# Layer 0's recurrence on pairs of chunks, memory attention on two row halves, an earlier page table and a new order in a two-layer decoder step

## The chip, the cores and the metric

The kernel runs on one core of a Trainium2 chip. The metric is the time of one execution on the device in microseconds (us). Of the kernel before three runs were timed, and one further execution was recorded by the profiler. TensorE is called PE below and its weight loads PEld; VectorE is DVE, ScalarE is ACT, GpSimd is POOL, and SyncE is SP.

## The reference

One step of a decoder with two layers, for a prompt of 512 tokens and 8 samples of 4 tokens (544 columns in all). Layer 0 mixes tokens by a gated linear recurrence, layer 1 by attention over keys that an indexer selects; beside the mixer each layer attends with 4 heads to 256 memory tokens, and each layer ends with a gated MLP that has a convolution over three tokens. The recurrence, which the change rewrites, is by chunks of 32 tokens and heads of 128:

```python
HGRN_CHUNK = 32
def step(S, inp):
    qc, kc, vc, gc = inp
    b = jnp.cumsum(gc, axis=2)
    b_last = b[:, :, -1:, :]
    q_dec = qc * jnp.exp(b)
    k_dec = kc * jnp.exp(-b)
    scores = jnp.where(causal, jnp.einsum('bhtk,bhsk->bhts', q_dec, k_dec), 0.0)
    o = jnp.einsum('bhtk,bhkv->bhtv', q_dec, S) + jnp.einsum('bhts,bhsv->bhtv', scores, vc)
    S_new = (jnp.exp(b_last[:, :, 0, :])[..., None] * S
             + jnp.einsum('bhsk,bhsv->bhkv', kc * jnp.exp(b_last - b), vc))
    return S_new, o
```

Six such heads stand side by side, the prompt has 16 chunks in each, and the state after the last chunk is an output too.

## The kernel before

Activations lie feature-major in tiles of 128 rows and 544 columns (32 of the samples, then 512 of the prompt). The weights come as 199 units of 128x1024, loaded by SP's queue up to three units ahead. `Weights._cut` splits each into two parts: `whi` by ACT, and `wlo` (the rest) by DVE or by POOL, whichever a planner's clock finds free. A projection (`fm`, `proj_fm`, `mm3`) adds three products of the parts, so the groups `a<-hi,whi`, `a<-lo,whi` and `a<-hi,wlo` make up most of PE's work. Every instruction is issued by one helper, so nearly all carry the same line, L398; they are told apart by the names of the tiles that they write and read.

The order of the instructions is not written out by hand. The program is a main line of projections with Python generators beside it (`Pump`), each a piece of work that yields what it must wait for. A planner (`Model`) keeps a clock for each engine by estimated costs, and decides between two main-line products which generator goes on; priorities stand in `PRI`, thresholds in `MAIN0`, `LEAD0`, `SLACK` and `BUSY`, and the main line of layer 0 in `MIX`: a number is a head's two projections, "hi" the values of two heads, "mem" the keys and values of the memory (`mkv` on PE), "g" a gate.

The parts that the change touches:
- `hgrn_head`, one generator for each of the six heads. A block is 128 tokens, that is 4 chunks; a head has 4 blocks. `front` makes the block's scores (`sc`) and the turned keys and then, on DVE, `km`: four masked copies of those, one for each chunk. `middle` makes 4 products `u` of 128x128 with all 128 rows at work, of which the mask leaves 32, and steps the state four times on DVE (`st`). `back` makes the output `ho`: the masked scores times the values, plus for each chunk the queries times the state before it, a product on 32 columns of PE. `ot` and `ots` turn the normed output.
- `mem_prompts`: four generators, each for two heads of memory attention and two tiles of tokens. The scores `ms` use 64 rows of PE (the head's 64 features). Then come the softmax, the turn `mpt` and the product `mo` into 64 columns.
- `out_proj` and `Norm`: the output projection adds into the stream `x`; behind each of its 8 feature blocks come `hi`, `lo`, a square and the sum `sqa`. `Norm._finish` sums the squares over features on PE (`st__finish`), takes the inverse root by 13 small DVE instructions (`m__finish`, `rs`), and spreads it by 5 PE transposes (`rb__finish`); the MLP's first results can only leave PSUM after that.
- The page table of layer 1's cache: 9 small DMAs issued on ACT's queue into `ptb` and `ptv`, and DVE instructions that turn them into row numbers (`iidx`, `vidx`). They stand in the program behind `out_proj`.

In the profile each full float32 product is two passes, so `u_hgrn_head ... x8` is 4 products.

## Time and profile before

| | us |
|---|---|
| median of 3 runs | 1495.1 |
| lowest and highest run | 1492.55, 1497.12 |
| span of the profiled execution | 1500.7 |
| PE busy in it | 1434.9 (96%), 11314 passes |
| DVE, ACT, POOL busy | 803.2, 587.5, 567.3 |
| mean granted clock of PE | 0.98 |

The profiled execution has no other time than its span, which is 5.6 us over the median. Busy PE means that some matmul was under way: ends of matmuls are modelled, so a stretch with a cold clock is busy too. The granted clock is the share of full speed (1.00 is 2.4 GHz, 0.50 is 1.2 GHz). Layer 0's mixer runs from the start to about 340 us, its MLP to about 700, layer 1's mixer to about 1100, and its MLP to the end.

### The profile page before, as it was taken

The page shows a single profiled execution, that of the slowest core. Times are in us where ns is not written, and L with a number is a line of the kernel's source. Part 1 is how long each engine was busy: PE and PEld are TensorE (multiplying, and loading weights), DVE is VectorE, ACT ScalarE, POOL GpSimd, SP SyncE. Part 2 cuts the span into 40 slices and gives each one's busy share as a digit, 9 for nine tenths or more (in the row PEclk, how much of TensorE's full clock was granted, in tenths as well). Part 3 has the DMA queues.
Part 4 walks back from the last instruction along what each step waited for, and adds up shares of the span by engine and source line. Part 5 has one row for each costly group of instructions (what it writes and reads, how often), then busy time and mean ns, then how long its engine had stood idle before and what let it go on. Part 6 is the DMA issues. An engine that isn't in the chain of part 4 may idle for free.

```text
span 1500.7 us, 28191 instructions
## 1 busy us (share of the span) xinstructions
PE 1434.9 (96%) x11314; PEld 1345.6 (90%) x11314; DVE 803.2 (54%) x1762; ACT 587.5 (39%) x1064; POOL 567.3 (38%) x600
## 2 busy tenths in 40 slices
PE   8989999998999999999999797689999999999998
PEld 7978889998999999999987775456999999999998
DVE  7466886653444234444469988867444442244431
ACT  5447466332333123333335443466333331133320
POOL 4422444323444124446753444341134440144410
PEclk9999999999999999999999997989999999999999
DMA  5542132321333223224414236631222323232241
GB/s 186 177 156 64 59 117 86 101 85 62 88 95 93 92 73 94 90 85 126 135 54 131 83 115 202 199 127 57 71 76 89 96 85 99 73 95 87 85 121 57
DMA packets 60145, 152.52 MB, mean 102 GB/s; under 512 B 9040, under 2 KB 22960, under 8 KB 60016
## 3 DMA queue, kind: packets, MB, share of 16 engines
q1 hardware_dynamic: 39456, 110.11, 23.9%
q0 software_dynamic: 8208, 26.50, 5.4%
q10 hardware_dynamic: 12352, 14.13, 2.9%
q8 instruction: 89, 1.46, 0.4%
q14 instruction: 40, 0.33, 0.1%
HBM read 142.23 MB, written 8.47 MB: 100 GB/s over the span
## 4 chain that ended last, share of the span: by engine, by line
PE 84%; DVE 11%; issue 2%; ACT 1%; DMA 1%; another core or an unknown queue 0%; ACTq 0%; POOL 0%; SPq 0%; DVEq 0%; POOLq 0%
PE a L398 71%; DVE ple_choose_sample L398 2%; PE u_hgrn_head L398 1%; DVE isc_index_prompt L398 1%; PE id_index_prompt L398 1%; PE mkv L398 1%; PE ao_prompt_attn L398 1%; PE ho_hgrn_head L398 1%; PE ms_prompt L398 1%; PE hgrn_head_samples L398 1%; PE as_prompt_attn L398 1%; DVE t L398 1%; DMA ptv<-pt 1%; DVE lo L398 1%; PE mo_prompt L398 1%
## 5 line engine op out<-in xcount | busy, mean ns | idle before, releaser
L398 PE MATMUL a<-hi,whi 128*128 128x272 f32 x2640 | 556.4, 292 | 1.4 <-DVE t L398 1.0
L398 PE MATMUL a<-lo,whi 128*128 128x272 f32 x2640 | 551.0, 290 | 4.9 <-DVE lo L398 4.6
L398 POOL TENSOR_TENSOR wlo<-raw,whi 128x1024 fp32r<-128x1024 f32 x143 | 342.7, 2397 | 557.3 <-ACT whi L398 551.1
L398 PE MATMUL a<-hi,wlo 128*128 128x272 f32 x2640 | 549.1, 289 | 0.0
L398 PEld LDWEIGHTS a<-hi,whi 128*128 128x128 f32 x2640 | 417.7, 190 | 9.2 <-issue 5.4
L398 PEld LDWEIGHTS a<-lo,whi 128*128 128x128 f32 x2640 | 418.1, 190 | 6.2 <-DVE lo L398 5.6
L398 PEld LDWEIGHTS a<-hi,wlo 128*128 128x128 f32 x2640 | 418.1, 190 | 0.0
L398 ACT ACTIVATE whi<-raw 128x1024 fp32r<-128x1024 f32 (+1 forms) x202 | 209.5, 1038 | 230.9 <-PE a L398 151.3
L398 DVE TENSOR_TENSOR wlo<-raw,whi 128x1024 fp32r<-128x1024 f32 (+1 forms) x59 | 79.7, 1351 | 160.6 <-ACT whi L398 157.7
L398 DVE TENSOR_TENSOR sc<-a,rb 128x544 f32<-128x544 f32 x53 | 38.4, 724 | 116.1 <-PE a L398 114.5
L398 DVE SCALAR_TENSOR_TENSOR conv<-ext,params,conv 128x560 f32<-128x560 f32 x88 | 70.6, 802 | 45.1 <-ACT conv L398 43.6
L398 DVE TENSOR_TENSOR ext<-a,rb 128x240 f32<-128x240 f32 x132 | 37.5, 339 | 105.9 <-PE a L398 102.2
L398 ACT ACTIVATE conv<-ext,params 128x560 f32<-128x560 f32 x44 | 37.6, 855 | 136.2 <-DVE ext L398 132.6
L398 ACT ACTIVATE hi<-sc 128x544 fp32r<-128x544 f32 x44 | 29.0, 658 | 137.3 <-DVE sc L398 137.3
L398 DVE TENSOR_TENSOR x<-a,x 128x544 f32<-128x544 f32 x48 | 34.7, 723 | 80.1 <-PE a L398 72.5
L398 POOL TENSOR_TENSOR sqa<-sqa,sq 128x544 f32<-128x544 f32 x24 | 34.8, 1448 | 110.0 <-ACT sq L398 108.3
L398 DVE TENSOR_TENSOR sc<-sc,conv 128x512 f32<-128x512 f32 x88 | 62.5, 748 | 4.9 <-DVE sc L398 0.5
L398 ACT ACTIVATE conv<-conv 128x560 f32<-128x560 f32 x44 | 29.6, 672 | 73.8 <-DVE conv L398 73.8
L398 ACT ACTIVATE hi<-x,params 128x544 fp32r<-128x544 f32 x32 | 23.9, 745 | 70.4 <-DVE x L398 68.5
L398 DVE TENSOR_TENSOR lo<-sc,hi 128x544 fp32r<-128x544 f32 x44 | 31.9, 725 | 31.9 <-ACT hi L398 31.9
L398 PE MATMUL a<-whi,hi 128*128 128x256 f32 x160 | 46.8, 293 | 0.0
L398 PE MATMUL a<-whi,lo 128*128 128x256 f32 x160 | 45.1, 282 | 0.0
(406 smaller groups left out, 1931.9 us busy)
## 6 DMA issues: line engine op xcount, KB each, us to landing
raw<-w SPq DMA_DIRECT2D x177, 512.0 KB, 3.6
raw<-w POOLq DMA_DIRECT2D x21, 512.0 KB
k_sample_scores<-ckT SPq DMA_DIRECT2D x46, 128.0 KB, 3.5
ck_mem_samples<-cmkT ACTq DMA_DIRECT2D x16, 256.0 KB, 6.2
cv_mem_samples<-cmv ACTq DMA_DIRECT2D x16, 256.0 KB, 4.7
st_s<-hgrn_head_samples POOLq DMA_DIRECT2D x12, 256.0 KB
hgrn_head_samples<-hst SPq DMA_DIRECT2D x10, 256.0 KB, 3.5
ck_sample_scores<-ckT SPq DMA_DIRECT2D x18, 128.0 KB, 2.1
```

Of the source, the lines that this page charges most:

```text
L398: return f(*args, **kw)
```

## The change

**Recurrence.** `hgrn_head` keeps states for pairs of chunks (64 tokens): 8 states for a head instead of 16. The masked copies `km` are gone. `updates` makes two products per block, of rows 0 to 63 and of rows 64 to 127, which write two PSUM banks. `scores` has one more product (`k` by the second chunk's queries, 128x64) for the part inside a pair, and three more ACT copies. `outputs` works on two blocks at a time. Instructions of the six heads: `u` 96 to 48, DVE state steps 96 to 48, `km` 24 to none, ACT copies of 32x32 none to 48 and of 128x128 (`kt`) none to 24, `o` copies 24 to 12.

**Memory attention.** In layer 0 both heads of a generator make their scores in turn, on the two row halves and into two banks; in both layers `mo` takes the heads in turn.

**Page table.** The 9 DMA issues go ahead of head 3's projections, the DVE instructions ahead of `out_proj`.

**Order.** New constants for the planner in layer 0; in layer 1 and its MLP the old order is replayed from a written string (`SCRIPT`), and PE's rows there differ in `mo` alone. Who makes `wlo` changes too: DVE 59 to 33 of the units, POOL 143 to 169; the 26 that change hands are all in layer 0. In all, PE goes from 10445 to 10415 instructions, DVE from 1671 to 1593, ACT from 1003 to 1062, POOL from 605 to 629.

```diff
-KEEP, MAIN0, MAIN1 = 3, 5, 1
+KEEP, MAIN0, MAIN1 = 3, 1, 1
-LEAD0, LEAD1, POOLED = -1.0, -100.0, 0
+LEAD0, LEAD1, POOLED = -3.0, -100.0, 1
-MIX = "0 hi hi mem 1 2 3 4 hi 5 g g g g g g".split()
+MIX = "0 1 hi mem 3 4 hi 2 5 hi g g g g g g".split()
...
+            def scores(*es):
+                for e in es:
+                    sbs[e] = bank("ms")
+                for i in range(2):
+                    for e in es:
+                        T.matmul(sbs[e][:, 256 * i:256 * i + 256], tok(qs[j][0], 2 * tp + i)[prs[e], :],
+                                 kt[prs[e], 256 * j:256 * j + 256], start=True, stop=True, skip_group_check=True)
...
+            for es in [(0, 1)] if l == 0 else [(0,), (1,)]:
...
-        def front(blk):
-            cols = slice(NS + 128 * blk, NS + 128 * blk + 128)
-            sb = bank("sc")
-            T.matmul(sb[:, 0:128], kd[:, cols], q[:, cols], start=True, stop=True, skip_group_check=True)
-            T.transpose(sb[:, 128:256], k[:, cols], ident)
-            sc = scs[blk % 3]
-            V.copy_predicated(sc, cc("bcaus").bitcast(I32), sb[:, 0:128])
-            km = slot(name="km")
-            V.tensor_mul(v3(km[:, :512], 4, 128), sb[:, 128:256].unsqueeze(1).to_broadcast([128, 4, 128]),
-                         cc("cmask").unsqueeze(2).to_broadcast([128, 4, 128]))
-            st[blk] = sc, km
...
+        def scores(blk, sb):
+            cols = slice(NS + 128 * blk, NS + 128 * blk + 128)
+            T.matmul(sb[:, 0:128], kd[:, cols], q[:, cols], start=True, stop=True, skip_group_check=True)
+            T.matmul(v3(sb[:, 256:320], 2, 32), k[:, cols], v3(q[:, cols], 2, 64)[:, :, 32:64], start=True, stop=True,
+                     skip_group_check=True)
+            T.transpose(sb[:, 128:256], ku[:, 128 * blk:128 * blk + 128], ident)
+            sc = scs[blk % 3]
+            V.copy_predicated(sc, cc("bcaus").bitcast(I32), sb[:, 0:128])
+            for p in range(2):
+                S.activation(sc[64 * p:64 * p + 32, 64 * p + 32:64 * p + 64], sb[64 * p:64 * p + 32, 256 + 32 * p:288 + 32 * p], AF.Copy)
+            kt = kts[:, 128 * blk:128 * blk + 128]
+            S.activation(kt, sb[:, 128:256], AF.Copy)
+            st[blk] = sc, kt
...
+        def updates(blk, ub):
+            for p in range(2):
+                rows = slice(64 * p, 64 * p + 64)
+                T.matmul(ub[p], st[blk][1][rows], vv(blk)[rows], start=True, stop=True, skip_group_check=True)
...
+        scores(0, bank("sc"))
+        for n in range(1, 5):
+            yield [kts] if n != 3 else [kts, st[1][1]]
+            hb = bank("ho") if n == 3 else None
+            b = bank("sc" if n < 4 else "ho")
+            ub = b[:, 384:512], bank("u")[:, 0:128]
+            updates(n - 1, ub)
+            if n == 3:
+                outputs(0, hb)
+            if n < 4:
+                scores(n, b)
+            scan(n - 1, ub)
...
+        if hd == 3:
+            page_table()
...
+        pump.begin(SCRIPT)
```

VectorE at the end of layer 0's mixer, before: the last blocks of `out_proj`, the page table's row numbers, and the norm.

```order
L398 TENSOR_TENSOR x_89<-a_3986,x_89 128x544
L398 SCALAR_TENSOR_TENSOR lo_4037<-x_89,params_79,hi_4036 128x544
L398 TENSOR_TENSOR sqa_3520<-sqa_3520,sq_4038 128x544
L398 TENSOR_SCALAR iidx<-ptb,consts_81 64x32 x2
L398 TENSOR_SCALAR vidx<-ptv,consts_81 128x8
L398 TENSOR_SCALAR vidx<-vidx 128x8 x3
L398 TENSOR_SCALAR m__finish_1_4120<-st__finish_1_4111 128x5
L398 TENSOR_SCALAR m__finish_2_4122<-m__finish_1_4120 128x5
L398 TENSOR_SCALAR rs_4066<-m__finish_2_4122 128x5
```

VectorE there after the change, first the rows where the row numbers now stand (the last head's norm and its gate, `lo_gate`):

```order
L417 TENSOR_TENSOR o_hgrn_head_1_3212<-o_hgrn_head_1_3212,m_hgrn_head_6_3433 128x512
L417 TENSOR_SCALAR oss_hgrn_head_1_3214<-oss_hgrn_head_1_3214,m_hgrn_head_6_3433 128x128
L417 TENSOR_TENSOR sc_3375<-sc_3375,on_hgrn_head_1_3165 128x544
L417 TENSOR_SCALAR iidx<-ptb,consts_81 64x32 x2
L417 TENSOR_SCALAR vidx<-ptv,consts_81 128x8
L417 TENSOR_SCALAR vidx<-vidx 128x8 x3
L417 TENSOR_TENSOR lo_gate_1_3536<-sc_3375,hi_gate_1_3535 128x544
```

and then the rows about the norm:

```order
L417 TENSOR_TENSOR x_89<-a_3957,x_89 128x544
L417 SCALAR_TENSOR_TENSOR lo_4008<-x_89,params_79,hi_4007 128x544
L417 TENSOR_TENSOR sqa_3491<-sqa_3491,sq_4009 128x544
L417 TENSOR_SCALAR m__finish_1_4066<-st__finish_1_4057 128x5
L417 TENSOR_SCALAR m__finish_2_4068<-m__finish_1_4066 128x5
L417 TENSOR_SCALAR rs_4018<-m__finish_2_4068 128x5
```

What moved: `iidx` and `vidx` no longer stand between the last `sqa` and the norm's chain, but ahead of the output projection. On PE, between `st__finish` and `rb__finish` stand now 30 products of the MLP, before 54.

TensorE in the steps of one head (head 1 before; names with `sc`, `u` and `ho` are PSUM banks, `sct` the masked scores):

```order
L398 MATMUL ho_hgrn_head_1_992<-v_731,sct_324 128x128
L398 MATMUL ho_hgrn_head_1_992<-st_hgrn_head_1_897,sc_564 32x128 x3
L398 MATMUL sc_hgrn_head_4_999<-sc_564,kd_hgrn_head_1_584 128x128
L398 MATMUL sc_hgrn_head_4_999<-consts_80,k_hgrn_head_1_581 128x128
L398 MATMUL u_hgrn_head_3_1007<-v_734,km_hgrn_head_3_906 128x128 x4
L398 MATMUL ho_hgrn_head_2_1017<-v_731,sct_325 128x128
L398 MATMUL ho_hgrn_head_2_1017<-st_hgrn_head_1_897,sc_564 32x128
L398 MATMUL ho_hgrn_head_2_1017<-st_hgrn_head_2_913,sc_564 32x128 x3
L398 MATMUL u_hgrn_head_4_1026<-v_734,km_hgrn_head_4_1003 128x128 x4
```

and after the change (the first of a block's two half products is written into a corner of the bank that has `sc`, for the last block `ho`, and the second into `u`; both read `kt`):

```order
L417 MATMUL sc_hgrn_head_4_1094<-v_915,kt_hgrn_head_1_959 128x128
L417 MATMUL u_hgrn_head_3_1095<-v_915,kt_hgrn_head_1_959 128x128
L417 MATMUL ho_hgrn_head_1_1093<-v_912,sct_324 128x128
L417 MATMUL ho_hgrn_head_1_1093<-v_912,sct_325 128x128
L417 MATMUL ho_hgrn_head_1_1093<-st_hgrn_head_1_1012,sc_542 32x128
L417 MATMUL ho_hgrn_head_1_1093<-st_hgrn_head_1_1012,sc_540 32x128
L417 MATMUL ho_hgrn_head_1_1093<-st_hgrn_head_1_1012,sc_542 32x128
L417 MATMUL ho_hgrn_head_1_1093<-st_hgrn_head_1_1012,sc_540 32x128
L417 MATMUL ho_hgrn_head_1_1093<-st_hgrn_head_2_1035,sc_542 32x128
L417 MATMUL ho_hgrn_head_1_1093<-st_hgrn_head_2_1035,sc_540 32x128
L417 MATMUL sc_hgrn_head_4_1094<-sc_542,kd_hgrn_head_1_580 128x128
L417 MATMUL sc_hgrn_head_4_1094<-sc_542,k_hgrn_head_1_577 128x64
L417 MATMUL sc_hgrn_head_4_1094<-consts_80,b_hgrn_head_1_578 128x128
```

What moved: where 4 products `u` stood together now stand two, and the scores have a third row. With the new `MIX` the steps of heads 0 and 1 alternate: from head 0's first scores to the end of `mkv` there are 142 instructions, 48 of them `mkv`, and none of a projection.

GpSimd in the first stretch, before (`sqa` is the sum of squares of the first norm):

```order
L398 TENSOR_TENSOR sqa_119<-sqa_119,sq_147 128x544
L398 TENSOR_TENSOR sqa_119<-sqa_119,sq_168 128x544
L398 TENSOR_TENSOR sqa_119<-sqa_119,sq_189 128x544
L398 TENSOR_TENSOR sqa_119<-sqa_119,sq_214 128x544
L398 TENSOR_TENSOR sqa_119<-sqa_119,sq_233 128x544
L398 TENSOR_TENSOR sqa_119<-sqa_119,sq_252 128x544
L398 TENSOR_TENSOR wlo_271<-raw_113,whi_270 128x1024
```

and after:

```order
L417 TENSOR_TENSOR wlo_123<-raw_92,whi_122 128x256 x2
L417 TENSOR_TENSOR sqa_119<-sqa_119,sq_147 128x544
L417 TENSOR_TENSOR wlo_123<-raw_92,whi_122 128x256
L417 TENSOR_TENSOR sqa_119<-sqa_119,sq_168 128x544
L417 TENSOR_TENSOR wlo_123<-raw_92,whi_122 128x256
L417 TENSOR_TENSOR sqa_119<-sqa_119,sq_189 128x544
L417 TENSOR_TENSOR wlo_207<-raw_98,whi_206 128x1024
L417 TENSOR_TENSOR sqa_119<-sqa_119,sq_214 128x544
L417 TENSOR_TENSOR sqa_119<-sqa_119,sq_233 128x544
L417 TENSOR_TENSOR sqa_119<-sqa_119,sq_252 128x544
L417 TENSOR_TENSOR wlo_271<-raw_113,whi_270 128x1024
L417 TENSOR_TENSOR wlo_277<-raw_115,whi_276 128x1024
```

What moved: the first units' `wlo`, which DVE made before, stand between the sums of squares on GpSimd now.

## Rows read from the trace of the kernel before

**Rows 1.** Windows of several stretches: busy us (instructions) of PE, PEld, DVE, ACT, POOL; granted clock; DMA.

```profile
0.00:37.50 37.50, 31.24 (x194) 28.73 (x195) 27.57 (x56) 19.35 (x33) 18.36 (x28) 0.91 0.55 186
75.00:112.50 37.50, 33.35 (x260) 26.50 (x259) 24.87 (x61) 17.18 (x41) 10.88 (x9) 1.00 0.48 156
112.50:337.50 225.00, 222.85 (x1893) 205.58 (x1892) 155.58 (x372) 127.71 (x259) 83.80 (x73) 1.00 0.27 86
337.50:375.00 37.50, 32.45 (x247) 31.74 (x246) 14.61 (x41) 9.97 (x13) 12.69 (x13) 0.91 0.19 62
900.00:1000.00 100.00, 76.69 (x543) 52.96 (x543) 81.88 (x276) 47.39 (x125) 42.95 (x45) 0.83 0.57 182
```

**Rows 2.** Waits of TensorE from 0 to 375 us: total us, times, longest.

```profile
PE a L398 <- DVE lo L398: 4.6, 4, 2.3
PE u_hgrn_head L398 <- DVE km_hgrn_head L398: 2.2, 1, 2.2
PE ots_hgrn_head L398 <- DVE oss_hgrn_head L398: 1.6, 1, 1.6
PE ot_hgrn_head L398 <- DVE o_hgrn_head L398: 1.5, 1, 1.5
```

**Rows 3.** Timeline of VectorE and TensorE about 350 us: start, us, instruction, idle before.

```profile
349.65 0.23 DVE L398 TENSOR_SCALAR vidx<-ptv,consts 128x8 int32<-128x8 int32 x1 [10.00 <-DMA ptv<-pt]
...
352.57 1.36 PE L398 MATMUL rb__finish<-consts,rs 128*128 128x128 f32 x5 [5.05 <-DVE rs L398]
```

**Rows 4.** The same windows view, two stretches behind that wait.

```profile
352.50:360.00 7.50, 7.43 (x41) 6.98 (x42) 3.89 (x9) 2.82 (x6) 0.32 (x2) 0.68 0.01 2
360.00:367.50 7.50, 7.50 (x62) 7.50 (x61) 3.18 (x6) 3.11 (x5) 2.81 (x5) 1.00 0.24 72
```

**Rows 5.** Timeline of TensorE in the turns of the heads, 228.8 to 236 us.

```profile
229.10 1.05 PE L398 MATMUL u_hgrn_head<-v,km_hgrn_head 128*128 128x128 f32 x8
229.99 0.39 PE L398 MATMUL sc_hgrn_head<-sc,kd_hgrn_head 128*128 128x128 f32 x2
...
231.96 0.38 PE L398 MATMUL ho_hgrn_head<-v,sct 128*128 128x128 f32 x2
232.28 0.42 PE L398 MATMUL ho_hgrn_head<-st_hgrn_head,sc 128*32 128x128 f32 x6
232.62 0.49 PE L398 MATMUL sc_hgrn_head<-sc,kd_hgrn_head 128*128 128x128 f32 x2
```

**Rows 6.** Timeline of TensorE at the indexer of layer 1, about 802 us.

```profile
801.81 1.09 PE L398 MATMUL de_index_sample<-ckT,iqs 64*32 64x512 f32 x16
802.69 0.24 PE L398 MATMUL dn_index_sample<-ikn,iqs 64*32 64x32 f32 x8
```

**Rows 7.** Timeline of TensorE at the prompt's memory scores, layer 0.

```profile
114.36 3.72 PE L398 MATMUL ms_prompt<-mkt,mq 64*128 64x256 f32 x16
118.01 0.52 PE L398 MATMUL a<-hi,whi 128*128 128x272 f32 x2
...
121.65 1.13 PE L398 MATMUL ms_prompt<-mkt,mq 64*128 64x256 f32 x4
122.71 0.52 PE L398 MATMUL a<-hi,whi 128*128 128x272 f32 x2
```

**Rows 8.** Timeline of VectorE and GpSimd in the first 24 us.

```profile
5.24 0.78 DVE L398 SCALAR_TENSOR_TENSOR lo<-x,params,hi 128x544 fp32r<-128x544 f32 x1 [0.21 <-ACT hi L398]
...
10.27 1.89 DVE L398 SCALAR_TENSOR_TENSOR lo<-x,params,hi 128x544 fp32r<-128x544 f32 x1
...
10.22 3.15 POOL L398 TENSOR_TENSOR sqa<-sqa,sq 128x544 f32<-128x544 f32 x2 [0.16 <-ACT sq L398]
```

**Rows 9.** Costliest groups of the page: GpSimd's cuts of weights, mean ns.

```profile
L398 POOL TENSOR_TENSOR wlo<-raw,whi 128x1024 fp32r<-128x1024 f32 x143 | 342.7, 2397 | 557.3 <-ACT whi L398 551.1
```

**Rows 10.** Groups of ScalarE's copies out of PSUM, 0 to 375 us.

```profile
L398 ACT ACTIVATE o_hgrn_head<-ho_hgrn_head 128x128 f32<-128x128 f32 x24 | 6.6, 275 | 15.8 <-PE ho_hgrn_head L398 15.7
...
L398 ACT ACTIVATE hi_prompt<-mot_join 64x32 fp32r<-64x32 f32 x4 | 0.8, 192 | 2.4 <-DVE lo_prompt L398 2.2 <-PE mot_join L398 0.2
```

More of the change, by code (lines that the diff above doesn't have):

```diff
@@ L1 @@
+import re
 import numpy as np
@@ L366, in go @@
                 s = max(s, self.mine.get(n, 0.0))
+        if port:
+            s = next((b for a, b in self.port["pool" if eng == "dve" else "dve"] if a <= s < b), s)
+            self.port[eng] = [*self.port[eng][-15:], (s, s + cost)]
         e = self.t[eng] = s + cost
@@ L485, in cost @@
         c = 0.148 + n * 2.1 / 1000
-    model.go(eng, c, ins, outs)
+    wide = [v for v in aps if size(v) > 1 and v.tensor.name not in model.psum]
+    port = eng == "pool" or eng == "dve" and (len(wide) > 1 or fast)
+    model.go(eng, c, ins, outs, port)
 class Gen:
@@ L504, in make, with begin, play, pick @@
         self.names[name] = n = self.names.get(name, 0) + 1
-        return Gen(it, after, f"{name}{n}", pri, margin)
+        g = Gen(it, after, f"{name}{n}", pri, margin)
+        self.made.append(g)
+        return g
+    def begin(self, script):
+        self.made = [*self.gens, *self.dv]
+        self.script = iter([c for n, c in re.findall(r"(\d*)(\D)", script) for _ in range(int(n or 1))])
+    def play(self):
+        for c in self.script:
+            if c == ".":
+                return
+            g = self.made[LETTERS.index(c)]
+            self.step(g, self.gens if g in self.gens else self.dv)
+    def pick(self, c):
+        return c if self.script is None else next(self.script) == "+"
     def add(self, it, after=None, pri=5, margin=0):
@@ L569, in run @@
     def run(self, *need):
+        if self.script is not None:
+            return self.play()
         while True:
@@ L600, in finish @@
     def finish(self, g):
+        if self.script is not None:
+            return self.play()
         while not g.done:
@@ L610, in space @@
     def space(self, tag):
+        if self.script is not None:
+            return self.play()
         m = self.m
@@ L620, in drain @@
     def drain(self):
+        if self.script is not None:
+            return self.play()
         while self.gens:
@@ L1323, in middle @@
                 state[0] = s1
-            st[blk] = sc, ns, states
-        def back(blk):
-            sc, ns, states = st.pop(blk)
-            ob = bank("ho")[:, 0:128]
-            T.matmul(ob, sc, vv(blk), start=True, stop=False, skip_group_check=True)
-            for c in range(4):
-                if states[c] is not None:
-                    n = NS + 32 * (4 * blk + c)
-                    T.matmul(ob[32 * c:32 * c + 32], q[:, n:n + 32], states[c], start=False, stop=True,
-                             skip_group_check=True)
-            S.activation(o[:, 128 * blk:128 * blk + 128], ob, AF.Copy)
-            S.activation(oss[:, 384:512], ob, AF.Square, accum_out=ss[:, blk:blk + 1])
+            st[blk] = st[blk][0], ns, states
@@ new lines, in outputs @@
+        def outputs(first, hb):
+            for j in range(2):
+                T.matmul(hb[:, 128 * j:128 * j + 128], st[first + j][0], vv(first + j), start=j == 0, stop=False,
+                         skip_group_check=True)
+            for j in range(2):
+                blk = first + j
+                for c in range(4):
+                    i, s0 = 2 * blk + c // 2, st[blk][2][c // 2]
+                    if s0 is not None:
+                        qc = qs[:, 32 * i:32 * i + 32] if c % 2 else q[:, NS + 64 * i:NS + 64 * i + 32]
+                        T.matmul(hb[32 * c:32 * c + 32, 128 * j:128 * j + 128], qc, s0, start=False, stop=True,
+                                 skip_group_check=True)
+            S.activation(o[:, 128 * first:128 * first + 256], hb[:, 0:256], AF.Copy)
+            for j in range(2):
+                S.activation(oss[:, 384:512], hb[:, 128 * j:128 * j + 128], AF.Square, accum_out=ss[:, first + j:first + j + 1])
@@ L1592, in program @@
         V.tensor_scalar(vidx[:, i, :], vidx[:, 0, :], float(i), None, op0=ALU.add)
+    norm = Norm(gffn[:, 0, :])
+    out_proj(0, cat, [*([g] for g in gates), [mg[0], mg[1], mg[4]], mg[2:5]], norm)
+    n1 = Norm(gmix[:, 1, :])
     def gather(out, src, idx):
@@ L1615, in program @@
     norm = n1
+    if plan is not None:
+        pump.begin(SCRIPT)
     h = norm.h
```

155 lines of the change are left out of this document (87 added, 68 removed).

## The prediction

> **What bounds the kernel now.** I began with the stretches of the program, since the share of busy time is a mean over parts with different limits. TensorE is the bound nearly everywhere: between 112.5 and 337.5 us, where layer 0's heads and gates run, it is busy for 222.85 of 225 us at the full granted clock [rows 1]. There a microsecond taken off TensorE is a microsecond off the time, and one taken off VectorE is worth nothing. What TensorE does not fill lies at three places that the change touches. In the first 37.5 us it is busy for 31.24, and around the end of layer 0's mixer (337.5 to 375) for 32.45, both at a granted clock of 0.91. The list of what TensorE waits for then names the rest: the first projection waits 4.6 us for `lo` of the input, and the heads' steps have three single waits, for `km` (2.2), `oss` (1.6) and `o` (1.5) [rows 2].
>
> The largest single stall is the page table's. VectorE runs its instructions in order; `vidx` stands there ahead of the norm's chain and waits 10.00 us for its load, so that the norm's 13 small instructions start late and TensorE's `rb__finish` stands still for 5.05 us [rows 3]. Behind it the clock is cold: 41 passes in the next 7.5 us at a granted clock of 0.68, and 62 in the 7.5 us after that at 1.00 [rows 4].
>
> **The change part by part.**
>
> *Page table.* The 9 DMAs go out at head 3 and `vidx` runs ahead of `out_proj`, long after they land. The wait of 5.05 goes, and with it the cold clock, (62 - 41) passes at 7.50/62 = 0.121 us: 2.5. What is late next is the norm's own chain. From the start of `vidx` to `rb__finish` it took 352.57 - 349.65 = 2.9 us with `vidx` in it [rows 3]; the changed order has 30 products between `st__finish` and `rb__finish`, 30 x 0.121 = 3.6 us, so it is covered, with 0.7 us to spare. Term: **-7.5**; if the clock dips anyway, -5.05. On ACT's queue the 9 issues now stand in front of a head's work; ACT is busy for 127.71 of 225 us there [rows 1], so I take 0, and the most that it could cost is the 10 us that VectorE waits today.
>
> *State updates `u`.* Today 8 passes take 229.99 - 229.10 = 0.89 us a block [rows 5], 0.111 a pass. After it there are two half products of two passes. Whether two row halves run side by side, the heads' trace does not show. The nearest rows are the indexer's products on 64 rows by 32 columns: 16 passes of 512 columns in 0.88 us [rows 6], although one pass of 256 columns on 64 rows takes 0.216 us (below); so parts of the array do run side by side. I take two half products for the time of one, 0.22. To that comes going into the 64-row mode and out of it: for `ms`, 16 passes take 3.65 us and 4 take 1.06 [rows 7], so a pass is (3.65 - 1.06)/12 = 0.216 and a visit 1.06 - 4 x 0.216 = 0.20. That is 0.42 against 0.89, for 24 blocks **-11.3**. If the halves run one after the other it is 0.64, and -6.0.
>
> The Trainium skill ("TensorEngine Tiling (Array Packing)", Key Properties) says that a change of tiling mode drains TensorE, which speaks against this edit; the 0.20 us of a visit agrees. The same section has tiles load and multiply in parallel, and its Gotcha 1 adds that row tiles may not share a PSUM bank at the same time; here the halves have two banks, and by that rule the sum is the one with -11.3.
>
> *The part inside a pair.* One more product in the scores, two passes at the 0.111 of `u`: 0.22 for each of 24 blocks, **+5.3**. Its moving side has only 64 columns, so it could be half, +2.7; I take the dear end, as the stationary side that must be loaded is whole.
>
> *Outputs `ho`.* A block takes 232.62 - 231.96 = 0.66 us [rows 5]. Two blocks together save one of two visits to the 32-column mode. No row prices that visit alone; with the 0.20 above, 12 pairs save **-2.4**; at the other end nothing.
>
> *Memory scores in layer 0.* 32 passes in five visits take 3.65 + 4 x 1.06 = 7.9 us. After it: three visits, and two heads side by side, 16 x 0.216 + 3 x 0.20 = 4.1: **-3.8**. If the halves run in turn, 7.5: -0.4. `mo` in layer 1 is not counted: there the second head comes late anyway.
>
> *`wlo` on GpSimd.* 26 cuts go from VectorE to GpSimd, at 2.4 us each [rows 9]. With units cut ahead they are hidden in the dense stretches, not at the start. There a `lo` takes 0.78 us alone and 1.89 beside GpSimd's `sqa` [rows 8], 1.1 more, and TensorE waits for `lo`. With GpSimd now cutting the first unit's blocks too, all eight `lo` of the first norm could meet it: 8 x 1.1 = 8.8 us at worst; none if the cuts that leave VectorE make up for it. I take **+3**, nearer to the free end because VectorE loses as many cuts from its own queue.
>
> The Trainium skill ("GPSIMD Engine Reference", Specifications) has GpSimd's SBUF interfaces shared with VectorE, in contention when a VectorE instruction has two SBUF inputs. The 0.78 and 1.89 agree; by that rule each two-input `lo` beside a cut pays the 1.1, which is the 8.8 above, and the sum would be 5.8 us worse.
>
> *Waits in the heads' steps.* The three old ones, 2.2 + 1.6 + 1.5 = 5.3, go, since `km` is gone and another order stands around `ot`. In their place each step waits for ACT to copy `kt` and two corners: 0.275 + 2 x 0.19 = 0.66 us by the nearest copies [rows 10]. Heads 2 to 5 have projections to fill it. Heads 0 and 1 alternate with only `mkv` between them: 8 steps at some 0.5, 4.0. Term: **-1.3**, between -5.3 (all covered) and 0 (none).
>
> *At nothing.* `km` and half the state steps leave VectorE, which TensorE covers (VectorE is busy for 155.58 of 225 us [rows 1]); the 62 instructions more on ACT fit into its idle 97 us. Layer 1 keeps its order.
>
> Sum: -7.5 - 11.3 + 5.3 - 2.4 - 3.8 + 3 - 1.3 = **-18.0 us**. The profiled span of 1500.7 would be 1482.7; it lies 5.6 over the median of the runs, so the median goes from 1495.1 to **1477.1**.
>
> **The rivals.**
>
> *More is covered.* No wait in the steps and no contention at the start: -18.0 - 4.0 - 3 = -25.0, 1470.1. For it: only one step in the old heads waited at all. Against it: the alternating heads have no projection beside them.
>
> *Row halves run in turn.* `u` -6.0 and `ms` -0.4: -18.0 + 5.3 + 3.4 = -9.3, 1485.8. For it: the side-by-side rows that I have also split the columns, and no row splits the rows alone.
>
> *GpSimd's queue becomes the wait.* Each head needs `k` from GpSimd early on; if that stands behind a cut, 2.4 us are lost on each of six heads, 14.4: -3.6, 1491.5, which no measurement would tell from no change (I take 0.3%, 4.5 us, as the bound; 1490.6 and 1499.6). With half of it, 1484. For it: 26 cuts more in that queue. Against it: GpSimd is busy for only 83.80 of 225 us [rows 1].
>
> *Slower: the alternating heads cool the clock.* The 142 instructions from head 0's first scores to the end of `mkv` are some 220 passes, at 33.35/260 = 0.128 us [rows 1] about 28 us. If the steps' waits leave TensorE so idle that it is granted 1.2 GHz there, they cost up to 28 more: +10.0, 1505.1. It decides from 18.0/28 = 64% of the stretch at the low level, and is over 0.3% from 80%. For it: 900 to 1000 us, busy 77%, clock 0.83 [rows 1]. Against it: 75 to 112.5 us, the place in question, busy 89% at a clock of 1.00.
>
> **How the numbers follow.** Forecast (1472 to 1484) 0.52; more covered 0.15; halves in turn 0.14; GpSimd's queue 0.13, half of it below 1490.6; cold clock 0.06. Faster: 0.52 + 0.15 + 0.14 + 0.06 = 0.87; same 0.08, the rest of GpSimd's case and a little of the cold clock; slower 0.05. The range takes in the ends of the unknown costs: down to 1466 (the first rival with the cheap end of the added product, and a little), up to 1490 (halves in turn and a part of GpSimd's wait). Outside are about 0.15.
>
> **What would show it.** No wait of `rb__finish`, and a granted clock near 1.00 from 337.5 to 375 us. Two half products of `u` and the way into the next full product in about 0.42 us, against 0.64 in turn. `ms` on 16 passes in 16 x 0.108 + 0.2 = 1.9 us against 3.65. `lo` at the start above 1 us. The granted clock where `mkv` and heads 0 and 1 stand. I am wrong if layer 0's mixer does not end some 10 us earlier, or if waits on ACT or GpSimd in it sum to more than 10 us.

## The result and the profile after

The changed kernel takes 1506.1 us (median of 4 runs, 1505.84 to 1508.65) against 1495.0: a ratio of 1.0086, interval 1.0066 to 1.0106. The forecast was 1477.1, faster; it is slower by 11 us. One number of before needs a word: its recorded execution was longer than its kind. A run's time lies 1.7 us over its span in the recording of after (1505.84 and 1504.1), and the kernel before, recorded again, spans 1489.6 (e0 below). Most of the difference is in layer 1 (350.6 and 336.7 us, e0 below); the mixer of layer 0 is the shorter one in the first recording, 339.4 us against 342.9.

The windows view of after answers to [rows 1]; the first row is the whole mixer of layer 0, up to the sums of the norm (`st__finish`, called "the sums" below).

```profile
0.00:352.50 352.50, 327.80 (x2626) 291.23 (x2626) 203.88 (x461) 194.00 (x418) 164.38 (x152) 0.96 0.35 110
75.00:112.50 37.50, 32.55 (x253) 22.82 (x252) 20.90 (x70) 19.89 (x69) 18.24 (x16) 0.82 0.44 140
80.00:90.00 10.00, 7.92 (x38) 6.02 (x39) 6.43 (x17) 3.78 (x13) 6.80 (x5) 0.50 0.22 63
112.50:337.50 225.00, 212.98 (x1752) 192.72 (x1751) 135.84 (x309) 127.42 (x282) 95.42 (x80) 0.98 0.27 82
337.50:375.00 37.50, 37.50 (x305) 37.21 (x304) 14.27 (x34) 14.12 (x19) 16.46 (x16) 1.00 0.30 90
```

The end of the mixer did what was forecast: from 337.5 to 375 us TensorE is busy throughout at the full clock, where it had 32.45 us and 0.91. The loss that both recordings of before show is in the mixer itself. It lasts 352.5 us to the norm's sums; before, the same point is at 339.4:

```profile
0.00:339.40 339.40, 326.84 (x2691) 296.91 (x2692) 225.89 (x526) 180.49 (x358) 129.72 (x135) 0.99 0.35 114
```

So TensorE is idle for 352.5 - 327.8 = 24.7 us in place of 12.6, and busy for 327.8 in place of 326.8, although passes were taken away: the granted clock is 0.96 in place of 0.99, and 0.50 from 80 to 90 us. Of the 13.1 us that the mixer grew, 12.1 are idle time.

Against the second recording of before (342.9 us, 13.2 idle) it is 9.6 us longer and idle for 11.5 us more. That comparison shows the rest of the program too: from the mixer's sums to those behind the MLP it takes 401.0 us against 407.0, and from there to the sums behind layer 1's mixer 350.1 against 340.9, although TensorE's order there is the old one but for `mo`. The first recording had 354.8 for that last stretch, so how much of it is the change's cannot be read from single recordings.

Who TensorE waited for (answers to [rows 2]; the first eight):

```profile
PE ot_hgrn_head L417 <- DVE o_hgrn_head L417: 5.0, 2, 3.2
PE a L417 <- POOL wlo L417: 3.6, 2, 2.8
PE mob_mem_samples L417 <- ACT mpt_mem_samples L417: 2.3, 2, 2.1
PE hgrn_head_samples L417 <- DVE st_hgrn_head L417: 1.6, 2, 1.3
PE u_hgrn_head L417 <- DVE hgrn_head_samples L417: 1.6, 2, 1.4
PE ots_hgrn_head L417 <- DVE oss_hgrn_head L417: 1.5, 1, 1.5
PE mpt_mem_samples L417 <- ACT mp_mem_samples L417: 1.3, 2, 1.1
PE sc_hgrn_head L417 <- ACT kt_hgrn_head L417: 1.3, 2, 0.8
```

The list is long and flat: the wait for `lo` at the start (4.6) became one for `wlo` on GpSimd (3.6), `ot` waits 5.0 instead of 1.5, and each of the heads' and the samples' steps waits a little. `km` and `rb__finish` are gone from it. Outside the mixer the one wait that is clearly new is that of `rb__finish` at the end of the MLP, 3.1 us. On the copies of `kt` by ACT, which the forecast priced, TensorE waits 1.3 us. At the start nothing is lost or won: TensorE is busy for 31.27 of the first 37.5 us, before for 31.24, and the eight `lo` take 0.78, 0.78, 1.08, 0.79 and, the last four together, 7.53 us, in all 11.0, against 0.78, 0.78, 1.89, 0.78 and 7.17 before, 11.4.

What stands behind `ot` is seen in the timelines of VectorE and GpSimd at that moment:

```profile
115.67 0.17 DVE L417 TENSOR_TENSOR m_hgrn_head<-m_hgrn_head,m_hgrn_head 128x5 f32<-128x5 f32 x1
115.87 2.36 DVE L417 SCALAR_TENSOR_TENSOR m_hgrn_head<-m_hgrn_head,m_hgrn_head 128x5 f32<-128x5 f32 x1
118.26 0.17 DVE L417 TENSOR_TENSOR m_hgrn_head<-m_hgrn_head 128x5 f32<-128x5 f32 x1
```

```profile
115.86 2.35 POOL L417 TENSOR_TENSOR wlo<-raw,whi 128x1024 fp32r<-128x1024 f32 x1 [0.84 <-ACT whi L417]
```

An instruction on 128x5 numbers takes 2.36 us in place of 0.17, from the moment at which GpSimd's cut begins until it ends (115.86 + 2.35). The same stands ahead of the new wait in the MLP's end:

```profile
754.91 1.76 DVE L417 TENSOR_SCALAR m__finish<-m__finish 128x5 int32<-128x5 int32 x1
...
757.51 2.41 DVE L417 TENSOR_TENSOR m__finish<-rs 128x5 f32<-128x5 f32 x1
```

```profile
754.24 2.40 POOL L417 TENSOR_TENSOR wlo<-raw,whi 128x1024 fp32r<-128x1024 f32 x1
...
757.54 2.35 POOL L417 TENSOR_TENSOR wlo<-raw,whi 128x1024 fp32r<-128x1024 f32 x1
```

Two cuts on GpSimd, two instructions of the norm's chain held, 1.76 and 2.41 us. The contention that the prediction priced for `lo` at the start [rows 8] meets short chains on VectorE that have TensorE waiting at their end.

### The profile page after: what moved, and what is told of

Its sections match the earlier page's. It is cut to its first block, busy times and chain, and to the rows that moved or that the text cites. A ratio compares the mean times of both kernels' runs of the same rounds, so it can differ in the third digit from the quotient of the medians.

```text
span 1504.1 us, 28106 instructions
## 1 busy us (share of the span) xinstructions
PE 1435.1 (95%) x11254; PEld 1340.9 (89%) x11254; DVE 771.6 (51%) x1684; ACT 600.6 (40%) x1123; POOL 620.6 (41%) x624
## 3 DMA queue, kind: packets, MB, share of 16 engines
q1 hardware_dynamic: 39456, 110.11, 24.2%
## 5 line engine op out<-in xcount | busy, mean ns | idle before, releaser
L417 POOL TENSOR_TENSOR wlo<-raw,whi 128x1024 fp32r<-128x1024 f32 (+1 forms) x169 | 400.4, 2369 | 562.4 <-ACT whi L417 553.5
L417 DVE TENSOR_TENSOR wlo<-raw,whi 128x1024 fp32r<-128x1024 f32 x33 | 45.8, 1388 | 115.2 <-ACT whi L417 115.2
L417 DVE TENSOR_TENSOR sc<-a,rb 128x544 f32<-128x544 f32 x59 | 42.7, 723 | 120.0 <-PE a L417 118.5
L417 DVE TENSOR_TENSOR ext<-a,rb 128x240 f32<-128x240 f32 x132 | 37.5, 340 | 108.9 <-PE a L417 105.0
```

Source lines behind the costliest of these rows:

```text
L417: return f(*args, **kw)
```

## The experiments

Ratios are to the kernel before, run on the same chip in the same job; the jobs ran on chips that differ by 1.4%, so ratios are compared and not times.

| kernel | ratio | interval |
|---|---|---|
| the change | 1.0086 | 1.0066 to 1.0106 |
| e1, cuts back on VectorE | 1.0030 | 1.0013 to 1.0048 |
| e4, cuts back in the MLP alone | 1.0054 | 1.0036 to 1.0072 |
| e5, before with the new cuts | 1.0103 | 1.0080 to 1.0126 |
| e2, before with the page table moved | 0.9982 | 0.9969 to 0.9995 |
| e12, the same, order planned anew | 1.0092 | 1.0075 to 1.0110 |
| e13, the change with the table late | 1.0158 | 1.0139 to 1.0176 |
| e3, the change, old constants | 1.0164 | 1.0142 to 1.0187 |
| e6, e1 with the old heads | 1.0063 | 1.0042 to 1.0085 |
| e8, before with the new heads | 1.0080 | 1.0061 to 1.0099 |
| e9, e1 with head 1 after the memory | 1.0126 | 1.0108 to 1.0145 |
| e11, e1 with head 3 before the memory | 1.0048 | 1.0030 to 1.0066 |
| e7, e2 with the new memory attention | 1.0328 | 1.0305 to 1.0350 |
| e10, e2 with 23 more cuts on VectorE | 1.0080 | 1.0053 to 1.0106 |

**e0, the kernel before recorded again.** No edit. 

> The kernel before, unchanged, recorded once more. Its recorded execution spanned 1500.7 us, while a span of the changed kernel lies 1.74 us below its run time, so the median of 1495.1 should stand for a span near 1493.3. If the two waits of 4.1 and about 3 us in layer 1 (near 976 and 1006 us, at the softmax weights' turns) belong to that one execution, the span here is 1493 to 1495 and they are gone, while the page table's wait of rb__finish stays near 5 us. If they belong to the kernel, the span is near 1500 again.

The span is 1489.6, and `rb__finish` waits 5.1 us again. Layer 1 lasts 336.7 us from its `rb__finish` to the next sums, 350.6 in the first recording, with the same order: the waits of 4.1 and 3 us there belonged to that execution. Of the 11.1 us between the two spans, layer 1 makes 13.9, while the mixer of layer 0 is 3.5 us longer here.

**e1, the cuts back.**

```diff
+ON_DVE = {0, 1, 3, 8, 13, 14, 15, 21, 22, 30, 31, 34, 35, 36, 37, 38, 39, 63, 64, 66, 67, 68, 70, 71, 72, 96, 97, 98, 99, 100, 101, 102, 103}
...
-                (V if pump.pick(model.t["dve"] <= late) else G).tensor_sub(lo[:, c:c + n], raw[:, c:c + n], hi[:, c:c + n].bitcast(F32))
+                e = V if pump.pick(model.t["dve"] <= late) else G
+                if u < 104:
+                    e = Engine(nc.vector if u in ON_DVE else nc.gpsimd, e._n, e._m, e._c)
+                e.tensor_sub(lo[:, c:c + n], raw[:, c:c + n], hi[:, c:c + n].bitcast(F32))
```

The planner still accounts for the old choice, so that every instruction keeps its place and only the engine of the cut changes. 

> The changed kernel with its order of instructions kept, and the cuts of layer 0's weights made by the engine that made the cut of the same place before (26 units back from GpSimd to VectorE). Theory A (a cut on GpSimd, 2.4 us, holds up VectorE instructions that run beside it, and so the short chains on which TensorE waits): the waits for wlo (3.6), o (5.0), oss (1.5) and rs (3.1) fall by half or more, the cold stretches with them, time 1493 to 1498. Theory B (the new order of the heads leaves TensorE without work and cools its clock, whoever cuts): 1502 to 1507, with the stretch from 73 to 90 us still at a granted clock of 0.5.

The median is 1497.4: theory A for 0.56% (8.4 us, some 4 to 12 by the two intervals), and theory B for what is left. The cold stretch is still there (80 to 90 us at 0.67). `ot` waits 1.0 us here and `rb__finish` not at all, but `oss` still 1.5, the wait of 3.6 for `wlo` at the start is one of 4.6 for `lo` again, and TensorE's idle time in the mixer is 24.2 us, against 24.7: the cuts are not what makes it idle. Between the two recordings 3.1 us are in the mixer, 3.3 at the MLP's end and 5.4 in layer 1, whose order is the same. Two recordings of one kernel differ by more than that in the mixer (3.5) and in layer 1 (13.9), so of this split only the MLP's end, where the held instructions are seen, can be put down to the cuts.

**e5, the mirror.** The same edit in the kernel before, with the changed kernel's list.

```diff
+ON_DVE = {14, 16, 66, 67, 70, 71, 98, 99, 101, 102}
...
+                if u < 104:
+                    e = Engine(nc.vector if u in ON_DVE else nc.gpsimd, e._n, e._m, e._c)
```

> The mirror: the kernel before, its order kept, with the cuts of layer 0 made by the engine that makes the cut of the same place in the changed kernel (GpSimd has more of them). If cuts on GpSimd cost by themselves, whatever the order: 7 to 11 us more than the kernel before, 1500 to 1504. If they cost only in the changed order, where VectorE's short chains happen to meet them: 1492 to 1496.

1.0103, about 15 us and beyond the first case: the cuts cost by themselves, in an order that has nothing else of the change. TensorE's waits show two lines of after again, one at the start and one at the MLP's end:

```profile
PE a L399 <- POOL wlo L399: 3.6, 2, 2.8
...
PE rb__finish L399 <- DVE rs L399: 3.1, 1, 3.1
```

In the mixer `ot` waits 2.2 us instead of 1.5. Where the rest of the 15 us is, the trace does not show: the recorded execution took 1498.97 us, the shortest of the six.

**e4, the MLP's cuts alone.** In e1:

```diff
-                if u < 104:
+                if 36 <= u < 104:
```

> The changed kernel, order kept, with the cuts given back to VectorE (by place, as before) in layer 0's MLP alone: 12 units more on VectorE there; the mixer's cuts stay on GpSimd. The run with all cuts back lay 8.7 us below the changed kernel, and its profile has 3.1 of that in the mixer, 3.3 between the MLP's end and rb__finish and 5.4 in layer 1. If the MLP's cuts make the last two (GpSimd late with the page gathers at the MLP's end, then cutting beside the norm's chain): 1497 to 1499, no wait of rb__finish at 760 us. If the mixer's cuts are what matters: 1502 to 1504.

1.0054, between the two cases: some 0.32% of e1's 0.56% come from the 12 units of the MLP, though nothing waits inside it. The intervals of e4 and e1 and those of e4 and the change overlap at their ends, so the split is rough. One sign of the first case failed: `rb__finish` still waits 1.9 us at the MLP's end. Each cut there is made by the engine that made it before, and the last instruction of the norm's chain is held all the same:

```profile
765.48 2.34 POOL L418 TENSOR_TENSOR wlo<-raw,whi 128x1024 fp32r<-128x1024 f32 x1 [1.00 <-ACT whi L418]
765.49 2.36 DVE L418 SCALAR_TENSOR_TENSOR rs<-m__finish,rs 128x5 f32<-128x5 f32 x1
```

In the kernel before (e0) the same two instructions start the other way round, 0.01 us apart, and the last one takes 0.17:

```profile
753.66 0.17 DVE L398 SCALAR_TENSOR_TENSOR rs<-m__finish,rs 128x5 f32<-128x5 f32 x1
753.67 2.40 POOL L398 TENSOR_TENSOR wlo<-raw,whi 128x1024 fp32r<-128x1024 f32 x1 [1.01 <-ACT whi L398]
```

So a part of the price at this place is a matter of hundredths of a microsecond. The recording shows one thing more: its mixer has the cuts and the order of after and takes 360.7 us, 8.2 longer, at a granted clock of 0.94 (the recorded execution, 1513.43 us, was the longest of the nine). A single recording tells a mixer's length to some 8 us and no better.

**e2, the page table alone.** The DMAs and the small instructions are issued at their new places, and the planner accounts for them at the old ones; TensorE and GpSimd keep their order row for row.

```diff
+        if hd == 3:
+            page_table()
...
-    V.tensor_scalar(vidx[:, 0, :], ptv, 64.0, cc("iota16"), op0=ALU.mult, op1=ALU.add)
+    PV.tensor_scalar(vidx[:, 0, :], ptv, 64.0, cc("iota16"), op0=ALU.mult, op1=ALU.add)
```

Here `PV` only counts, and `nc.vector` issues the same line ahead of `out_proj`. 

> The kernel before with the page table's load at head 3 and its row numbers ahead of the output projection, every other instruction in its old place. By the prediction's term: 7.5 us less than the kernel before, 1487.5, rb__finish without a wait. Rival: the wait in the one recorded execution was longer than usual, or the norm's chain is late anyway: 1490 to 1494.

0.9982, 2.7 us (0.7 to 4.6), in the rival's range by the ratio. `rb__finish` still waits 1.3 us. At the place itself the recording has more: `st__finish` to the next sums, 744.5 - 344.05 = 400.5 us against 749.9 - 342.9 = 407.0. It is the only kernel here that beats the one before, and the best.

**e13, the table late again in the changed kernel.** The reverse of e2, order kept: the old places only count, and the late ones issue.

```diff
-        S.dma_start(ptb, bass.AP(tensor=pt_ap.tensor, offset=pt_ap.offset, ap=[[0, 128], [1, 64]]))
+        PS.dma_start(ptb, bass.AP(tensor=pt_ap.tensor, offset=pt_ap.offset, ap=[[0, 128], [1, 64]]))
...
     n1 = Norm(gmix[:, 1, :])
+    nc.scalar.dma_start(ptb, bass.AP(tensor=pt_ap.tensor, offset=pt_ap.offset, ap=[[0, 128], [1, 64]]))
```

> The changed kernel with the page table's DMAs and row numbers back behind the output projection, every other instruction in its place (30 products between st__finish and rb__finish). By the prediction's term 7.5 us more than the changed kernel, a ratio of 1.0136 to the kernel before; with fewer products to cover the wait it should be 3 us dearer still at the place (24 x 0.125), 1.0155. If the table is worth only the 3.1 us that its move gave in the kernel before: 1.0107.

1.0158 against 1.0086, 0.72% or 10.8 us (some 7 to 15 by the intervals), the dearest of the three cases. From the mixer's sums to the next ones the recording has 411.6 us where after has 401.0, 10.6 more at the place itself. `rb__finish` waits 8.7 us:

```profile
PE rb__finish L417 <- DVE rs L417: 8.7, 1, 8.7
```

So in the changed kernel, where 30 products cover the wait and not 54, the move is worth the term of 7.5 us and probably more. Why the runs show only 2.7 of some 6 us in the old order is open; layer 1 was 3 us longer in e2's recording than in e0's, and its length differs between recordings of one kernel by more than that.

**e12, the same move, planned anew.** e2 with the planner told of the move.

```diff
-        nc.scalar.dma_start(ptb, bass.AP(tensor=pt_ap.tensor, offset=pt_ap.offset, ap=[[0, 128], [1, 64]]))
+        S.dma_start(ptb, bass.AP(tensor=pt_ap.tensor, offset=pt_ap.offset, ap=[[0, 128], [1, 64]]))
...
-    PV.tensor_scalar(vidx[:, 0, :], ptv, 64.0, cc("iota16"), op0=ALU.mult, op1=ALU.add)
```

> The kernel before with the page table moved, as in the run that gave a ratio of 0.998, but with the planner told of the move: the same instructions, and an order drawn anew from there (348 rows differ on TensorE). If an order that the planner draws anew loses by itself, because its estimated costs are not the chip's: a ratio of 1.004 to 1.012 (6 to 18 us over the kernel before). If the lost time is in the changed work: 0.996 to 1.000, as with the old order.

1.0092, that is 1.1% above e2, with the same work: what differs is the order, and two cuts that the planner gave to VectorE. The mixer's sums stand at 355.4 us in place of 344.0, 11.4 later; the rest is in layer 1, which has no written order here. (The two ran on different chips. That the chip makes little of the mixer's length is likely, and not shown: e13's sums, from the job of e12, stand at 353.9 and the change's own at 352.5, but e4's at 360.7.) The two mixers, e12 and then e2:

```profile
0.00:355.40 355.40, 334.76 (x2691) 301.25 (x2692) 239.00 (x532) 180.03 (x358) 127.98 (x135) 0.97 0.34 110
```

```profile
0.00:344.00 344.00, 327.72 (x2691) 296.09 (x2692) 229.52 (x531) 181.34 (x359) 130.96 (x136) 1.00 0.35 113
```

As many passes (2691), but TensorE is idle for 20.6 us against 16.3, 4.3 more, and busy for 334.8 against 327.7, 7.0 more, at a lower clock. The planner goes by estimated costs, and this order has TensorE waiting at places where the old one did not: `ho` waits 1.5 us, in e2 for nothing, and `ot` 3.5 against 1.5.

The other recordings agree. In the old order TensorE is idle in the mixer for 12.6 us (before), 13.2 (e0), 16.3 (e2) and 15.0 (e5). In each of the eight orders that the planner drew anew it is idle for more, whichever heads and constants they have: 20.6 (e12), 21.8 (e7), 23.7 (e8), 24.7 (the change), 25.5 (e6), 27.6 (e11), 36 (e3) and 38 (e9). The one exception is the old order with more cuts in VectorE's queue, 26.1 (e10).

**e3, the old constants** in the changed kernel.

```diff
-KEEP, MAIN0, MAIN1 = 3, 1, 1
+KEEP, MAIN0, MAIN1 = 3, 5, 1
-LEAD0, LEAD1, POOLED = -3.0, -100.0, 1
+LEAD0, LEAD1, POOLED = -1.0, -100.0, 0
-SLACK = 2
+SLACK = 0.5
...
-MIX = "0 1 hi mem 3 4 hi 2 5 hi g g g g g g".split()
+MIX = "0 hi hi mem 1 2 3 4 hi 5 g g g g g g".split()
```

`BUSY` and `PRI` are the old ones too. 

> The changed kernel with the planner's constants and the main line of the kernel before (MIX, PRI, MAIN0, LEAD0, POOLED, SLACK, BUSY as they were); pairs of chunks, memory scores side by side, page table and the planner's cost formulas as changed. This undoes the order and most of the moved cuts together. Theories A and B both: 1482 to 1492, since the terms for the page table (-7.5), u, sc, ho and ms are left. If the rewritten recurrence itself is what costs (its waits on ACT's copies, visits to the 64-row mode dearer than 0.20): 1495 to 1505.

1.0164 (1518.1), beyond even the dear case. The old constants are no return to the old order: the planner has other work and other cost formulas, and its plan has `ot` waiting 12.7 us.

**e6 and e8, the heads.** e6 puts the old `hgrn_head` into e1; e8 puts the new one into the kernel before, with `MAIN0 = 1`. Both change the work, so the planner draws a new order in each. The core of e6, in `hgrn_head` (e8 is the reverse):

```diff
-        def scores(blk, sb):
...
-        def updates(blk, ub):
...
-        def scan(blk, ub):
...
-        def outputs(first, hb):
...
+        def front(blk):
...
+        def middle(blk):
...
+        def back(blk):
```

> The changed kernel with all cuts back (1497.4) and the old heads: states for each chunk, km and all, in the planner's new constants and main line. It tells the rewritten recurrence from the order. If the order costs and the recurrence gains (by the prediction's terms, -8.4 without the waits): slower than 1497.4, 1501 to 1506. If the recurrence's waits on ACT's copies and the dearer visits to the 64-row mode eat its gain, and the order is harmless: 1488 to 1494.

1.0063 (1503.8) against e1's 1.0030, the first case: with the constants of the change the new heads seem to gain some 5 us, though the two intervals overlap at their ends. TensorE's idle time in the mixer is 356.6 - 331.1 = 25.5 us with the old heads and 24.2 in e1: so the waiting is there without the new heads. 

> The kernel before with the rewritten recurrence alone (and MAIN0 = 1, as it needs one tile more); main line, priorities, cuts by rule, page table and memory scores as before. By the prediction's terms for u, sc and ho, 8.4 us less: 1484 to 1487. If each step waits for ACT's copies of kt and the corners, as in the run with the old order (1518): 1500 to 1515, with TensorE's idle time at ot, ho and the samples' products.

1.0080 (1505.8), the second case, with 354.1 - 330.4 = 23.7 us idle in the mixer. But e12 has nearly as much loss from a new plan alone, and in e8 the planner drew layer 1 anew as well, so e8 does not tell the heads' own waits from the plan's.

**e9 and e11, the stretch of heads 0 and 1.** Two other main lines in e1.

```diff
-MIX = "0 1 hi mem 3 4 hi 2 5 hi g g g g g g".split()
+MIX = "0 hi mem 1 3 4 hi 2 5 hi g g g g g g".split()
...
+MIX = "0 1 hi 3 mem 4 hi 2 5 hi g g g g g g".split()
```

> The changed kernel with all cuts back (1497.4), and head 1's projections behind the values and the memory's keys (0 hi mem 1 3 4 hi 2 5 hi in place of 0 1 hi mem 3 4 hi 2 5 hi), so that heads 0 and 1 no longer alternate with mkv alone between them. If that stretch is what the new order loses (waits and a granted clock of 0.5 from 77 to 90 us): 1490 to 1494, no stretch at 0.5 there. If the loss is spread over all six heads' steps: 1496 to 1503.

1.0126, dearer than either case; the waits moved to other places (`ot` 5.5 us, `mpt` 4.4, a load of the samples' memory 3.3). 

> The changed kernel with all cuts back (1497.4), and head 3's projections ahead of the memory's keys (0 1 hi 3 mem 4 hi 2 5 hi): heads 0 and 1 still alternate, now with 96 more products of a projection beside them. Stretch theory: 1490 to 1495, the clock at 1.00 from 77 to 110 us. Spread theory: 1496 to 1502.

1.0048, the second case, and no better than e1, though the stretch is now warm:

```profile
75.00:112.50 37.50, 32.76 (x284) 25.90 (x286) 17.58 (x46) 19.48 (x59) 17.16 (x14) 1.00 0.42 144
```

The clock is back at 1.00 from 75 to 112.5 us, and the whole mixer is no shorter (359.8 us, with 27.6 us of idle time and a granted clock of 0.95: the cold stretches are elsewhere). As this main line is a new plan too, what the cold stretch costs by itself is not shown; warming it in this way gained nothing.

**e7, the memory scores.** The new `mem_prompts` in e2's program.

```diff
-            for e in range(2):
-                h, pr = 2 * j + e, slice(64 * e, 64 * e + 64)
-                yield [rs, kt]
...
+            for es in [(0, 1)] if l == 0 else [(0,), (1,)]:
+                yield [rs, kt]
+                scores(*es)
```

> The kernel before with the page table moved (which alone came to 3.1 us less) and with the changed kernel's memory attention: scores of two heads side by side on the row halves. The old heads and the old constants stay; the planner plans anew, so other rows move too. By the prediction's term for the scores (-3.8; the changed kernel's trace has 7.9 us of passes fallen to 4.6, -3.3): 1486 to 1488. If two heads at a time only make ACT's softmax late: 1490 to 1495.

1.0328, in neither case, and it says nothing on the scores: layer 1 has no written order here, and its new plan takes 403 us between its two norms against 340 in e2. A new plan is the likely cause, as in e12, but its other work was not told apart here; the changed kernel's `SCRIPT` keeps layer 1 from it.

**e10, more cuts on VectorE.** e2 with all 36 cuts of the mixer and the output projection on VectorE, order kept.

```diff
+                e = V if model.t["dve"] <= late else G
+                if u < 36:
+                    e = Engine(nc.vector, e._n, e._m, e._c)
```

> The kernel before with the page table moved (1489.9) and all 36 cuts of layer 0's mixer and output projection on VectorE (23 of them on GpSimd before). If each cut on GpSimd costs some 0.4 us through VectorE (15 us for 26 in the mirror run), 23 fewer give 1480 to 1486. If the cost is in where the few of them meet a chain, and VectorE's own queue now delays it: 1489 to 1496.

1.0080, dearer than both cases: the other direction loses too. TensorE waits 6.4 us for `km` and 6.8 for `mp`, behind cuts in VectorE's own queue. Of the three divisions tried in the old order (e2, e5, e10), the old one is the best.

## Why the prediction was wrong, point by point

**The step that failed** is the one on waits in the heads' steps, -1.3 between -5.3 and 0. It took the old waits as gone and priced the new ones by ACT's copies, as if the order around them stayed. With new constants, cost formulas and work the planner drew the whole mixer anew, and TensorE's idle time there went from 12.6 us to 24.7, +12.1. The prediction's first sign of being wrong came with it: the mixer ends 13.1 us later, not some 10 earlier. Of the waits on ACT's copies that I priced at 4.0, the list has 1.3. e12 shows that a new plan alone, with the same work, costs 1.1% (11.4 us in the mixer, by one recording of each); e6, that TensorE idles as long with the old heads under the new constants; and all eight new orders idle longer than the old one. The lower clock came with it: 0.96 in place of 0.99 over 327 us of busy time is an estimated 9.8 us, which the sum had at nothing and one rival had in a single stretch. No rival of mine had a plan that loses by itself. The range allowed no positive value for the term, although nothing excluded one.

**Cuts on GpSimd: the right mechanism, the wrong place and size.** +3 was taken, and e1 measured +8.4. That this is near the bound of 8.8 is chance: the bound was worked out for eight `lo` at the start, and those take 11.0 us, before 11.4. The price that the trace shows fell due at `ot` and at the norm's small instructions at the MLP's end. e5 shows that the cuts cost in the old order too. "Hidden in the dense stretches" was true inside the MLP and failed at its edge. The rule of the Trainium skill that I weighed here ("GPSIMD Engine Reference", Specifications) is contention with a VectorE instruction that has two SBUF inputs or is in a mode that uses two ports. The trace agrees for two inputs at 128x5 (115.87: 2.36 us), and has an instruction on one input held as well (754.91: 1.76); whether that one was in such a mode no run here shows.

**State updates `u`: half right.** The two halves start 0.01 us apart and run side by side, but a pair takes 0.21 us, not 0.11. One block of after, with the products about it, whose first half product of each pass bears the name `sc` (answers to [rows 5]):

```profile
231.00 0.33 PE L417 MATMUL sc_hgrn_head<-sc,k_hgrn_head 128*128 128x64 f32 x2
231.17 0.28 PE L417 MATMUL sc_hgrn_head<-consts,b_hgrn_head 128*128 128x128 f32 x1
...
232.47 0.28 PE L417 MATMUL a<-whi,lo 128*128 128x256 f32 x1
232.59 0.28 PE L417 MATMUL a<-wlo,hi 128*128 128x256 f32 x1
232.80 0.37 PE L417 MATMUL sc_hgrn_head<-v,kt_hgrn_head 64*128 64x128 f32 x1
232.81 0.37 PE L417 MATMUL u_hgrn_head<-v,kt_hgrn_head 64*128 64x128 f32 x1
233.01 0.27 PE L417 MATMUL sc_hgrn_head<-v,kt_hgrn_head 64*128 64x128 f32 x1
233.02 0.27 PE L417 MATMUL u_hgrn_head<-v,kt_hgrn_head 64*128 64x128 f32 x1
233.22 0.71 PE L417 MATMUL ho_hgrn_head<-v,sct 128*128 128x128 f32 x4
233.87 0.63 PE L417 MATMUL ho_hgrn_head<-st_hgrn_head,sc 128*32 128x128 f32 x12
234.43 0.38 PE L417 MATMUL sc_hgrn_head<-sc,kd_hgrn_head 128*128 128x128 f32 x1
```

From 232.80 to 233.22 the two pairs take 0.42 us. The visit is as forecast: the product ahead takes 0.21 (232.59 to 232.80) in place of 0.12 (232.47 to 232.59), and coming out is about as dear (the first pass behind takes 0.21 in place of 0.11), 0.2 in all. So a block is at 0.6, not 0.42: (0.89 - 0.6) x 24 = -7.0, not -11.3. That is close to the rival in which the halves run in turn (0.64, -6.0): side by side, two pairs took no less than four passes of `u` in a row before, 4 x 0.111. `ho` takes 234.43 - 233.22 = 1.21 us for two blocks. It stands right behind a `u`, so some 0.1 of that is the way out of the 64-row mode, which the 0.6 has already; 1.11 against 1.32 is -2.5, as forecast (-2.4). The added product takes 231.17 - 231.00 = 0.17: +4.1, not +5.3.

**Memory scores: right in mechanism, nearly right in size.** 16 passes take 138.55 - 136.63 = 1.92 us, forecast 1.9; the two visits of 8 passes take 144.85 - 143.27 = 1.58 and 165.69 - 164.62 = 1.07:

```profile
136.63 2.00 PE L417 MATMUL ms_prompt<-mkt,mq 64*128 64x256 f32 x16
138.55 0.52 PE L417 MATMUL a<-hi,whi 128*128 128x272 f32 x2
...
143.27 1.61 PE L417 MATMUL ms_prompt<-mkt,mq 64*128 64x256 f32 x8
144.85 0.55 PE L417 MATMUL mpt_prompt<-consts,mp_prompt 128*128 128x128 f32 x3
...
164.62 1.13 PE L417 MATMUL ms_prompt<-mkt,mq 64*128 64x256 f32 x8
165.69 0.39 PE L417 MATMUL a<-whi,hi 128*128 128x256 f32 x1
```

That is 4.6 us where 7.9 stood: -3.3, forecast -3.8. So the work on TensorE fell by some -7.0 + 4.1 - 2.5 - 3.3 = -8.7 us, where -12.2 were forecast, and the 9.8 us of the lower clock took it back: TensorE is busy for 1.0 us more.

**Page table: right in mechanism**, no wait of `rb__finish` and a full clock behind it; 10.8 us in the changed kernel (e13) and 2.7 in the old (e2), against 7.5.

**The rival that cooled the clock** gave 1505.1 and the clock did fall where it said. That the time came out near it is chance: 0.82 over the 37.5 us from 75 is some 13.5 us at the lower level, half of the 28 and short of the 64%, and e11 warmed the stretch and gained nothing.

Put together for the changed kernel: +8.4 for the cuts (e1) and -10.8 for the page table (e13) leave 11.1 - 8.4 + 10.8 = +13.5 us for the new order and the rewritten work, if the two add. With 8.7 us of work saved, its waits and its clock cost some 22, as much as the idle time and the clock of the recording, 12.1 + 9.8 = 21.9, though a part of those is the cuts'. That is a remainder: no run kept the old order with the new heads, and so how much of it the heads' own waits on ACT make stays open.

## What to carry to other kernels

Where a planner or a scheduler sets the order, a change of its constants, its cost formulas or even the place of ten small instructions is a change of the whole order: price it by runs with the order held fixed (account at the old place, issue at the new), and keep a term for the new plan with its own range on the losing side. A busy engine can hide a move of work to a neighbour inside a dense stretch and still pay at the stretch's edge, where short chains of tiny instructions have the bottleneck waiting. And a bound that was worked out for one place of contention holds for that place only: list every short chain that the moved work can meet.

## What the runs showed of the hardware that I had not expected

An instruction on 128x5 numbers on VectorE took 2.36 us instead of 0.17 beside a cut on GpSimd: it ended only with the other engine's instruction, 0.02 us behind it. Two products on 64 rows by 128 columns ran side by side, yet a pair took 0.21 us, as long as two passes on all 128 rows one after the other, and no less than a pair on 256 columns, (1.92 - 0.20)/8 = 0.215. It took 0.01 us to decide such a meeting at the MLP's end: started just ahead of the cut, the instruction took 0.17 us (e0), just behind it 2.36 (e4). And the same order in layer 1 took between 336.7 and 350.6 us in two recordings of the same kernel.
